# Another order for the attention stage's buffers, and the softmax denominators' sum on GpSimd

## The chip, the cores and the metric

The kernel runs on one core of one Trainium2 chip, in one launch. The metric is the device time in microseconds (us), as the median of several runs; less is better. The engines are named as in the profile: PE (TensorE matmul), PEld (its weight loads), DVE (VectorE), ACT (ScalarE), POOL (GpSimd), SP (SyncE, which here only issues DMAs). A suffix q, as in SPq, marks the engine's own queue.

## The reference

Two layers over 2048 latent tokens and 256 context tokens, width 1024, all in float32. Layer 0 is a gated spatial mixer. Layer 1, which the change touches, is windowed attention with 16 query heads and 4 key/value heads of 64:

```
s_loc = q·k over the block and one block to each side (|i-j| <= 128), masked
s_ctx = q·k_ctx over all 256 context keys
p     = softmax([s_loc, s_ctx, sink])          # one sink logit for each head
o     = p_loc @ v + p_ctx @ v_ctx
x     = LN(alpha*x + gate * ((o * silu(z)) @ w_out))
```

The softmax's denominator of a row and head is the sum of its exponentials (`l` in the kernel) and the exponential of the sink logit, both taken against the row's extreme value (`nm`).

## The kernel before, in words

**Stages.** The gated mixer and its output projection, then a projection stage that makes q, k, v and z of layer 1 and writes them to DRAM scratch, then attention with the output projection and the last LayerNorm. Each float32 matmul is made of three (or two) matmuls of split operands, high and low parts; the splitting (`hi_act` at L122 on ACT, `lo_dve` at L125 on DVE, `lo_pool` at L128 on POOL) follows every product of PE that is multiplied again.

**Attention.** There are 16 blocks of 128 queries (`b`), and in each four units, one for each key/value head (`kv`), of four query heads (`hq`). A unit goes over its key tiles `j`: three local ones and two of the context, so 5 steps (4 in the first and the last block). A block is thus 20 steps. For each unit: `s_mm` (L1100 to L1103) makes the scores, `s_max` (L1111, DVE) masks them and takes the extreme, `s_exp` (L1119, ACT) the exponentials and their sum `l`; for each step `t_mm` (L1126) transposes four heads' tile on PE, `t_hi` (ACT) and `t_lo` (DVE, tile `pl`) split it, `pv_mm` (L1143, L1144) multiplies it with v two steps later. `o_copy` (L1149, ACT) and `o_add` (L1155, DVE) end a unit.

**The denominators.** They are made for half a block at a time (`hf`: units 0 and 1, or 2 and 3), by `z_den`. Stage 0 (L1166, DVE) subtracts, stage 1 (L1168, ACT) takes the sink's exponential, stage 2 adds `l` (L1170), takes the reciprocal (L1171) and transposes it (L1173), all on DVE, stores it to DRAM scratch `escr` (L1175) and loads it back spread over the partitions as `eb` (L1179), both through SP. The last stage multiplies z with it on POOL (L1182). Then `y_mul` (L1187, POOL) multiplies the attention output with z, `y_hi` (ACT) and `y_lo` (L128, POOL, tile `yl`) split it, and `out_piece` (L1220 to L1222, PE) projects it, spread over the block that follows. `fin` is the LayerNorm of a finished block; its stage 5 is L579 on ACT, and its stage 6 is two additions and multiplications of a whole 128x1024 tile on POOL (L582, L583) with the store of the result.

**The order.** Each of these calls is put on a list with a time in steps (`at(t, fn, ...)`), and the list, sorted by time, is the order in which PE, DVE, ACT and POOL each get their instructions; an engine does not pass one instruction by for another. SP's order is left to the framework. In a block of 20 steps, counted from its first step, `z_den` stage 2 stands at 5.65 (first half) and 15.65 (second half), `t_lo` at .8 and `s_max` at .9 of a step, `o_add` at 6.5, 11.5, 16.5 and 21.5, stage 6 of `fin` for the block before the last one at 5.25, `y_lo` of the first half at 19.1, and the first `out_piece` that uses it at 21.4, which is 1.4 in the next block.

**The buffers.** A `Region` is a row of buffer groups, laid out in SBUF in the order of its list. The attention stage's region `b2` lies over what the projection stage used: first, from byte 0, 14 buffers of 4 KB (`bigb`) that hold the projection's split inputs `kh` and `kl` of the last token groups, which PE reads until the stage's last matmul; from 56 KB on the region `a3` (gate, hT, xt0 and xt1 of 4 KB each, then yr, yh, yl, tmp, whe, wle of 2 KB tiles). A new tile waits for the users of the earlier tiles on its own bytes. What attention needs first from DRAM are the keys of unit 1 (`kw` tiles, loads L1087 and L1088), v (`vk`), q, and a last weight row with its gate (both in `x1`). The scores of unit 0 are made already in the projection stage.

Of the kernel before, what the change touches and what calls it, by code (L numbers as in the profile page):

```python
# [12 lines left out]
ALU = mybir.AluOpType  # L13
# [36 lines left out]
def kernel(  # L50
# [28 lines left out]
    V, S, G, T = nc.vector, nc.scalar, nc.gpsimd, nc.tensor  # L79
# [69 lines left out]
    def kk_of(g):  # L149
        return 4 if GROUPS[g][1] == 256 else 2  # L150
# [9 lines left out]
    def at(th, g, k):  # L160
        return th[g, k // kk_of(g)][:, k % kk_of(g)]
# [312 lines left out]
    def spatial(c, g, cd, ut, vh, vl):  # L474
        tn = GROUPS[g][1]
        wsT, add = cd["wsT"], cd["add"]
        gc = gcols[:, c:c + 1]
        yt = a2.tile([P, tn], F32, "y", f"y{c}_{g}")
        npr = tn // 256
        pss = [bank(f"psp{c}_{g}_{pr}") for pr in range(npr)]  # L480
        for j in range(2):
            for pr in range(npr):
                T.matmul(pss[pr][:, j * 256:j * 256 + 256], vh[:, pr * 2 + j],
                         wsT.rearrange("q s p -> q (s p)"), start=True, stop=False)
            for pr in range(npr):
                T.matmul(pss[pr][:, j * 256:j * 256 + 128], vl[:, pr * 2 + j], wsT[:, 0], start=False, stop=True)
        for pr in range(npr):
            psv = pss[pr].rearrange("p (j s t) -> p j s t", j=2, s=2)
            t1 = a2.tile([P, 2, P], F32, "t1", f"t1{c}_{g}_{pr}")
            V.scalar_tensor_tensor(t1, psv[:, :, 1], gc, add[:, :].unsqueeze(1).broadcast_to([P, 2, P]),  # L490
                                   op0=ALU.mult, op1=ALU.add)
            V.scalar_tensor_tensor(t1, psv[:, :, 0], gc, t1, op0=ALU.mult, op1=ALU.add)
            cs = slice(pr * 256, pr * 256 + 256)
            G.tensor_tensor(yt[:, cs], t1.rearrange("p j t -> p (j t)"), ut[:, cs], op=ALU.mult)
        return yt
# [28 lines left out]
    for si, (c, g) in enumerate(steps):  # L524
# [16 lines left out]
        if si > 0:  # L541
            pc, pg = steps[si - 1]
            yt = spatial(pc, pg, cds[pc], uzs[si - 1], *vprep[si - 1])
# [370 lines left out]
    t = 0.0  # L914
# [88 lines left out]
    for n in range(1, 5):  # L1003
# [3 lines left out]
        for k in range(KD):  # L1007
            e = s + step * (k + 1) + 0.1
# [11 lines left out]
    with tc.manual_schedule(engines=compute | {mybir.EngineType.SP}):  # L1020
        for _, _, fn, a in sorted(plan, key=lambda p: p[:2]):
# [5 lines left out]
    b1.close()  # L1027
    bigb.close()

    b2 = Region(tc, "b2", [("kw", 4), ("x1", 2), ("otmp", 2), ("vk", 5), ("S", 9), ("ph", 7), ("q", 2), ("z", 1),  # L1030
                           ("eb", 2), ("pl", 7), ("oT", 2), ("yh0", 1), ("yh1", 1), ("yl0", 1), ("yl1", 1), ("yt", 2),
                           ("nm", 2), ("l", 2), ("es", 2), ("et", 2)])
    psS = ctx.enter_context(tc.tile_pool(name="psS", bufs=2, space=PSUM, reuse_waits="tile"))
    psT = ctx.enter_context(tc.tile_pool(name="psT", bufs=2, space=PSUM, reuse_waits="tile"))
# [2 lines left out]
    def b2t(name, shape, tag, bufs=None, dt=F32):  # L1037
        return b2.tile(shape, dt, tag, name)
# [15 lines left out]
    def len_keys(b):  # L1054
        return 4 if b in (0, NB - 1) else 5
# [105 lines left out]
    def z_den(b, hf, stage):  # L1161
        d = blk[b]
        es = est[hf][:, 0:8].rearrange("p (e j) -> p j e", e=2)
        nm, ns, l = (t[:, 8 * hf:8 * hf + 8].rearrange("p (j e) -> p j e", e=2) for t in (d["nm"], nsink, d["l"]))
        if stage == 0:
            V.tensor_tensor(es, nm, ns, op=ALU.subtract)  # L1166
        elif stage == 1:
            S.activation(est[hf][:, 0:8], est[hf][:, 0:8], AF.Exp)  # L1168
        elif stage == 2:
            V.tensor_tensor(es, es, l, op=ALU.add)  # L1170
            V.reciprocal(est[hf][:, 0:8], est[hf][:, 0:8])  # L1171
            et = b2t(f"et{b}_{hf}", [P, 32], "et")
            V.transpose(et, est[hf])  # L1173
            scr = escr[2 * b + hf]
            ld(scr.rearrange("i h q -> (i h) q"), et)  # L1175
            d["eb", hf] = eb = b2t(f"eb{b}_{hf}", [P, 4, P], "eb")
            for e in range(2):
                src = scr[:, 4 * e:4 * e + 4].rearrange("i j q -> i (j q)").unsqueeze(0)
                ld(eb[64 * e:64 * e + 64], src.broadcast_to([64, 4, P]))  # L1179
        else:  # L1180
            z = d["z"][:, 4 * hf:4 * hf + 4].rearrange("p j (i q) -> p j i q", i=4)
            G.tensor_tensor(z, z, d["eb", hf].rearrange("p i (j q) -> p j i q", j=4), op=ALU.mult)  # L1182
# [148 lines left out]
    for b in range(NB):  # L1331
        e = block_step[b + 1] if b + 1 < NB else NS
        if b + 1 < NB:
            at(block_step[b] + 8, load_block, b + 1)
        at(e - 11, z_load, b)
        for hf in range(2):
            if hf and b == NB - 1:
                break
            zb = first_step[4 * b + 2 * hf] + 3.55
            for i, t in enumerate((0.15, 1.1, 2.1)):  # L1340
                at(zb + t, z_den, b, hf, i)
            at(zb + 4.6 if hf else e - 7, z_den, b, hf, 3)
        if b == NB - 1:
            continue
        for hf in range(2):
            z = e + (-2.1 if len_keys(b) == 5 else -1.6, 1.9)[hf]
            ks = (4 * hf, 4 * hf + 4)
            at(z + (-3, -0.1)[hf], y_mul, b, *ks)
            at(z + (0.7, 1.5)[hf], y_hi, b, *ks)
            at(z + (1.2, 2.0)[hf], y_lo, b, *ks)  # L1350
        o = e + (1.4 if len_keys(b) == 5 else 1.7)
        os = 1.2 if b < NB - 2 else 0.8
        for i in range(2 * KD):
            at(o + i * os + (0.3 if i >= KD else 0), out_piece, b, i)
        for hf in range(2):
            t = o + (KD * (hf + 1) - 1) * os + hf * 0.3
            at(t + 0.3, out_copy, b, hf)
            at(t + 0.8, out_add, b, hf)
            at(t + 2.3, fin, b, hf)
        t += 2.35  # L1360
        late = (1.1, 2.8, 3.2) if b < NB - 2 else (0.5, 0.6, 0.7)
        for i, dt in enumerate((0, 0.3) + late):
            at(t + dt, fin, b, 2 + i)
    b, e = NB - 1, NS
    for i, t in enumerate((-5.05, -4.7, -4.0, -1.6)):
        at(e + t, z_den, b, 1, i)
    at(e - 2.3, y_mul, b, 0, 4)
    at(e - 1.9, y_hi, b, 0, 4)
# [84 lines left out]
```

## Time and profile before

| | |
|---|---|
| median of 3 runs | 2802.15 us (2800.67 to 2805.03) |
| the profiled execution, its own time | 2803.22 us |
| its span, first to last instruction | 2801.4 us |
| attention, from 2160 us on | 641.4 us of the span |

The profile shows one execution. Its time is 1.07 us above the median, and 1.82 us of it lie around the span. Stretches are given in us from the span's start; attention's first blocks lie at 2160 to 2204, its even part (blocks of about 39.6 us) at 2204 to 2757, its end behind that.

### The profile page before, as it was taken

How to read it: one execution, taken by the hardware profiler on the slowest of the kernel's cores; microseconds unless marked ns; L12 is line 12 of the kernel's file. 1: busy time of each engine (PE TensorE's matmuls, PEld its weight loads, DVE VectorE, ACT ScalarE, POOL GpSimd, SP SyncE). 2: the span in 40 equal slices, each digit the busy share in tenths (PEclk: the TensorE clock that was granted, in tenths of full speed). 3: DMA queues.
4: the chain of work that ended last, by engine and by line, in shares of the span. 5: the costliest groups of instructions: out<-in, count | busy, mean ns of one | idle time of the engine just before them, and what ended most of it. 6: DMA issues, size and time to landing. Idle time of an engine off the chain costs nothing.

```text
span 2801.4 us, 37614 instructions
## 1 busy us (share of the span) xinstructions
PE 2745.6 (98%) x13896; PEld 2323.9 (83%) x13896; DVE 1625.0 (58%) x3210; ACT 948.8 (34%) x1863; POOL 642.0 (23%) x522
## 2 busy tenths in 40 slices
PE   6999999999999999999999999999999999999998
PEld 4788888888888888888888888888888888888887
DVE  8612214666556665556545555545424888888887
ACT  4411211112211211223111112322213777777775
POOL 6000001322222222221011112122100334333343
PEclk9999999999999999999999999999999999999999
DMA  6422312322322322236333336633334544444442
GB/s 226 147 76 83 89 53 80 101 80 90 112 82 84 101 92 80 83 97 194 101 117 113 114 126 208 215 128 116 114 130 139 155 132 131 120 130 124 131 121 69
DMA packets 280717, 328.06 MB, mean 117 GB/s; under 512 B 24275, under 2 KB 192595, under 8 KB 280534
## 3 DMA queue, kind: packets, MB, share of 16 engines
q1 hardware_dynamic: 241652, 305.61, 34.0%
q10 hardware_dynamic: 38882, 20.05, 2.5%
q8 instruction: 109, 1.79, 0.3%
q14 instruction: 74, 0.61, 0.1%
HBM read 221.76 MB, written 103.83 MB: 116 GB/s over the span
## 4 chain that ended last, share of the span: by engine, by line
PE 87%; DVE 6%; DMA 3%; ACT 1%; issue 1%; POOL 0%; SPq 0%; DVEq 0%; ACTq 0%; POOLq 0%
PE pu L380 5%; PE pu L381 5%; PE pu L382 5%; PE pz L381 5%; PE pz L382 5%; PE pz L380 5%; PE po L622 5%; PE po L623 5%; PE po L625 5%; PE pt L744 4%; PE pt L745 4%; PE pt L743 4%; PE pv L244 4%; PE pv L242 4%; PE pv L243 4%; PE pT L1126 4%
## 5 line engine op out<-in xcount | busy, mean ns | idle before, releaser
L125 DVE TENSOR_TENSOR pl<-pT,ph 128x512 fp32r<-128x512 f32 x312 | 214.4, 687 | 78.4 <-ACT ph L122 74.6
L242 PE MATMUL pv<-wvh,hh 128*128 128x512 f32 x576 | 229.1, 398 | 16.5 <-ACT hh L122 16.5
L380 PE MATMUL pu<-hh,wuh 128*128 128x512 f32 (+1 forms) x640 | 240.4, 376 | 0.0
L381 PE MATMUL pu<-hh,wul 128*128 128x512 f32 (+1 forms) x640 | 236.1, 369 | 0.0
L382 PE MATMUL pu<-hl,wuh 128*128 128x512 f32 (+1 forms) x640 | 235.7, 368 | 0.0
L380 PE MATMUL pz<-hh,wzh 128*128 128x512 f32 (+1 forms) x640 | 235.4, 368 | 0.0
L381 PE MATMUL pz<-hh,wzl 128*128 128x512 f32 (+1 forms) x640 | 235.4, 368 | 0.0
L382 PE MATMUL pz<-hl,wzh 128*128 128x512 f32 (+1 forms) x640 | 235.4, 368 | 0.0
L244 PE MATMUL pv<-wvh,hl 128*128 128x512 f32 x576 | 229.2, 398 | 5.6 <-DVE hl L125 5.6
L622 PE MATMUL po<-woh,yh 128*128 128x512 f32 x576 | 226.7, 394 | 2.6 <-ACT yh L122 2.6
L743 PE MATMUL pt<-kh,wbh 128*128 128x512 f32 (+1 forms) x592 | 228.8, 386 | 0.0
L744 PE MATMUL pt<-kh,wbl 128*128 128x512 f32 (+1 forms) x592 | 228.7, 386 | 0.0
L745 PE MATMUL pt<-kl,wbh 128*128 128x512 f32 (+1 forms) x592 | 228.6, 386 | 0.0
L243 PE MATMUL pv<-wvl,hh 128*128 128x512 f32 x576 | 227.7, 395 | 0.0
L623 PE MATMUL po<-wol,yh 128*128 128x512 f32 x576 | 225.0, 391 | 0.0
L625 PE MATMUL po<-woh,yl 128*128 128x512 f32 x576 | 221.8, 389 | 0.0
L471 POOL TENSOR_TENSOR u<-u,z 128x512 f32<-128x512 f32 (+1 forms) x80 | 107.8, 1348 | 487.2 <-DVE z L470 479.0
L1111 DVE CUSTOM_DVE_ANT_0 S<-pS,mask 128x640 f32<-128x640 f32 (+1 forms) x252 | 216.9, 861 | 2.5 <-PE pS L1103 2.5
L1119 ACT ACTIVATE S<-S,nm 128x640 f32<-128x640 f32 (+1 forms) x240 | 196.7, 819 | 56.5 <-DVE nm L1111 56.5
L122 ACT ACTIVATE ph<-pT 128x512 fp32r<-128x512 f32 x312 | 185.0, 593 | 69.3 <-PE pT L1126 67.3
L1126 PE MATMUL pT<-ident,S 128*128 128x128 f32 x1232 | 186.0, 273 | 10.5 <-DVE pl L125 8.4
L470 DVE SCALAR_TENSOR_TENSOR z<-z,pz 128x512 f32<-128x512 f32 (+1 forms) x80 | 50.5, 632 | 243.1 <-ACT z L469 243.0
(235 smaller groups left out, 6142.0 us busy)
## 6 DMA issues: line engine op xcount, KB each, us to landing
vscr<-vt ACTq DMA_DIRECT2D x72, 256.0 KB, 2.3
yr<-yscr SPq DMA_DIRECT2D x72, 256.0 KB, 3.1
ar<-in_dram SPq DMA_DIRECT2D x64, 256.0 KB, 2.7
vr<-vscr SPq DMA_DIRECT2D x64, 256.0 KB, 2.7
yscr<-y SPq DMA_DIRECT2D x64, 256.0 KB, 2.5
q<-qscr SPq DMA_DIRECT2D x64, 256.0 KB, 3.8
wor<-in_dram SPq DMA_DIRECT2D x46, 256.0 KB, 2.7
kh<-khscr SPq DMA_DIRECT2D x56, 192.0 KB, 3.7
```

The source lines that it names most:

```text
L242: T.matmul(ps, hk[:, cs], wh, start=first, stop=False)
L243: T.matmul(ps, hk[:, cs], wl, start=False, stop=False)
L244: return T.matmul(ps, lk[:, cs], wh, start=False, stop=last)
L380: T.matmul(ps[:, 0:tn], w[0][:, k], at(hh, g, k), start=(k == 0), stop=False)
L381: T.matmul(ps[:, 0:tn], w[1][:, k], at(hh, g, k), start=False, stop=False)
L382: T.matmul(ps[:, 0:tn], w[0][:, k], at(hl, g, k), start=False, stop=(k == KD - 1))
L622: T.matmul(pss[hf], hi[:, c % 4], wh[:, cs], start=(c == 0), stop=False)
L623: T.matmul(pss[hf], hi[:, c % 4], wl[:, cs], start=False, stop=False)
L625: T.matmul(pss[hf], lo[:, c % 4], wh[:, cs], start=False, stop=(c == NC_A - 1))
L743: T.matmul(ps, wh[:, cs], at(kh, g, k), start=(k == 0), stop=False)
L744: T.matmul(ps, wl[:, cs], at(kh, g, k), start=False, stop=False)
L745: T.matmul(ps, wh[:, cs], at(kl, g, k), start=False, stop=(k == KD - 1))
```

## The change

The list of `b2` is put in another order: S, ph, pl, otmp and yt, which engines write, come first, over `bigb`; kw, vk, x1 and q, which DMAs write, come to lie from 58.5 to 90.5 KB, over `a3`. The sizes stay. In `z_den` the addition of `l` goes from DVE to POOL and stays at its place in the list as stage 2; the reciprocal, the transposition and the DMAs become stage 3, 0.9 steps later (6.55 and 16.55 in a block of 20 steps); the multiplication by POOL becomes stage 4, and for the second half goes from 18.15 to 18.85. In the last block the addition goes from -4.0 to -4.2 steps before the end and the rest to -3.9.

```diff
-    b2 = Region(tc, "b2", [("kw", 4), ("x1", 2), ("otmp", 2), ("vk", 5), ("S", 9), ("ph", 7), ("q", 2), ("z", 1),
-                           ("eb", 2), ("pl", 7), ("oT", 2), ("yh0", 1), ("yh1", 1), ("yl0", 1), ("yl1", 1), ("yt", 2),
+    b2 = Region(tc, "b2", [("S", 9), ("ph", 7), ("pl", 7), ("otmp", 2), ("yt", 2), ("kw", 4), ("vk", 5), ("x1", 2),
+                           ("q", 2), ("z", 1), ("eb", 2), ("oT", 2), ("yh0", 1), ("yh1", 1), ("yl0", 1), ("yl1", 1),
                            ("nm", 2), ("l", 2), ("es", 2), ("et", 2)])
...
         elif stage == 2:
-            V.tensor_tensor(es, es, l, op=ALU.add)
+            G.tensor_tensor(es, es, l, op=ALU.add)
+        elif stage == 3:
             V.reciprocal(est[hf][:, 0:8], est[hf][:, 0:8])
...
-            for i, t in enumerate((0.15, 1.1, 2.1)):
+            for i, t in enumerate((0.15, 1.1, 2.1, 3.0)):
                 at(zb + t, z_den, b, hf, i)
-            at(zb + 4.6 if hf else e - 7, z_den, b, hf, 3)
+            at(zb + 5.3 if hf else e - 7, z_den, b, hf, 4)
...
-    for i, t in enumerate((-5.05, -4.7, -4.0, -1.6)):
+    for i, t in enumerate((-5.05, -4.7, -4.2, -3.9, -1.6)):
         at(e + t, z_den, b, 1, i)
```

## Rows read from the trace of the kernel before

**Rows 1.** Stretches: us, busy us of PE, PEld, DVE, ACT, POOL; granted clock, DMA.
```profile
2160.00:2204.00 44.00, 36.97 (x226) 30.96 (x225) 34.84 (x79) 32.59 (x73) 12.52 (x8) 0.96 0.75 230
2204.00:2757.00 553.00, 544.62 (x3252) 474.71 (x3251) 480.49 (x1025) 429.23 (x881) 213.34 (x152) 1.00 0.41 123
```
**Rows 2.** Waits of PE, 2205 to 2770: us in total, times, longest.
```profile
PE pT L1126 <- DVE pl L125: 8.4, 13, 0.7
PE pO L1144 <- DVE pl L125: 0.6, 1, 0.6
```
**Rows 3.** Groups by line, DVE, 2205 to 2757: busy us, mean ns, idle before.
```profile
L1170 DVE TENSOR_TENSOR es<-es,l 128x8 f32<-128x8 f32 x28 | 32.4, 1158 | 0.0
```
**Rows 4.** The same view, POOL, 2205 to 2757.
```profile
L583 POOL TENSOR_TENSOR x<-x,st 128x1024 f32<-128x1024 f32 x13 | 30.9, 2378 | 1.0
L566 POOL TENSOR_TENSOR brs<-brs,mhalf 128x1 f32<-128x1 f32 x14 | 7.7, 551 | 16.7 <-DVE brs L562 16.7
```
**Rows 5.** Timeline, a first half: start, us, engine, line, [idle before, releaser].
```profile
2520.55 2.40 POOL L582 TENSOR_TENSOR x<-x,st 128x1024 f32<-128x1024 f32 x1 [2.26 <-ACT x L579]
2520.68 2.30 DVE L1170 TENSOR_TENSOR es<-es,l 128x8 f32<-128x8 f32 x1
2522.13 0.60 ACT L1149 ACTIVATE ot<-pO 64x512 f32<-64x512 f32 x1
2523.02 0.20 DVE L1171 RECIPROCAL es<-es 128x8 f32<-128x8 f32 x1
2523.03 2.38 POOL L583 TENSOR_TENSOR x<-x,st 128x1024 f32<-128x1024 f32 x1
2523.39 0.65 DVE L125 TENSOR_TENSOR pl<-pT,ph 128x512 fp32r<-128x512 f32 x1
2524.09 0.66 PE L1126 MATMUL pT<-ident,S 128*128 128x128 f32 x4 [0.66 <-DVE pl L125]
2526.57 0.39 PE L1144 MATMUL pO<-pl,v 128*128 128x512 f32 x1
```
**Rows 6.** Timeline, a second half, to the first use of `yl`.
```profile
2501.21 0.17 DVE L1170 TENSOR_TENSOR es<-es,l 128x8 f32<-128x8 f32 x1
2501.89 0.33 SPq L1175 DMA_DIRECT2D escr<-et  x1
2503.34 0.85 DVE L1155 TENSOR_TENSOR oT<-pO,ot 64x256 f32<-64x256 f32 x2
2507.94 1.29 POOL L1182 TENSOR_TENSOR z<-z,eb 128x512 f32<-128x512 f32 x1 [11.97 <-DMA eb<-escr]
2509.23 1.29 POOL L128 TENSOR_TENSOR yl<-oT,yh 128x512 fp32r<-128x512 f32 x1
2512.70 0.40 PE L1222 MATMUL pY<-wobh,yl 128*128 128x512 f32 x1
```
**Rows 7.** Timeline, `yl` and its first use one block earlier.
```profile
2471.35 1.31 POOL L128 TENSOR_TENSOR yl<-oT,yh 128x512 fp32r<-128x512 f32 x1
2473.12 0.40 PE L1222 MATMUL pY<-wobh,yl 128*128 128x512 f32 x1
```
**Rows 8.** Timeline where attention begins.
```profile
2160.40 0.32 SPq L1087 DMA_DIRECT2D kh<-khscr  x1
2161.26 0.69 DVE L836 SCALAR_TENSOR_TENSOR zt<-zt,pt 128x512 f32<-128x512 f32 x1 [3.76 <-ACT zt L834]
2162.74 0.36 PE L1100 MATMUL pS<-kh,q 128*128 128x256 f32 x1 [2.15 <-DMA kh<-khscr]
2163.41 0.58 PE L1101 MATMUL pS<-kl,q 128*128 128x256 f32 x1 [0.32 <-DMA kl<-klscr]
2164.46 0.75 DVE L1111 CUSTOM_DVE_ANT_0 S<-pS,mask 128x512 f32<-128x512 f32 x1 [2.51 <-PE pS L1103]
```
**Rows 9.** Stretch just behind: columns as in rows 1.
```profile
2163.00:2166.50 3.50, 3.18 (x15) 3.09 (x15) 1.32 (x3) 1.19 (x3) 0.00 (x0) 0.51 0.90 309
```
**Rows 10.** Timeline, waits inside the first block.
```profile
2174.33 0.95 DVE L1170 TENSOR_TENSOR es<-es,mask 128x8 f32<-128x8 f32 x1
2176.39 0.50 PE L1144 MATMUL pO<-pl,v 128*128 128x512 f32 x1 [1.50 <-DVE pl L125]
2201.06 0.63 ACT L122 ACTIVATE yh<-oT 128x512 fp32r<-128x512 f32 x1 [1.16 <-POOL oT L1187]
2202.96 0.50 PE L1144 MATMUL pO<-pl,vc 128*128 128x512 f32 x1 [0.20 <-DVE pl L125]
```

## The prediction

> **What bounds the kernel now.** I read the stretches first, then PE's waits, then the groups by line, then the timelines of one block, of the start of attention and of its first block. In attention's even part PE is busy for 544.6 of 553 us [rows 1]: what PE does not wait for cannot be won there. The list of its waits is short: 13 waits of up to 0.7 us and one of 0.6 us, 9.0 us together, all for `pl` of DVE [rows 2]. The reason stands in the groups: 28 additions of 128x8 numbers take 32.4 us [rows 3], though one takes 0.17 us [rows 6]. The timeline shows which are the long ones: the addition of the first half begins 0.13 us after POOL's L582 and ends with it, 2.30 us later [rows 5]. Half of them are like this; with 2.13 us lost in each, 28 x 0.17 + 13 x 2.13 = 32.5 us. Behind it `pl` comes late and PE idles 0.66 us [rows 5]. At the start of attention PE idles 2.15 and 0.32 us for the keys' loads, the first of which SP could issue only at 2160.40, behind the projection's last matmul [rows 8], and then runs for 3.5 us at a granted 0.51 [rows 9], the lower of the clock's two levels (1.2 GHz).
>
> **The layout.** The first keys come to lie over gate, hT and xt0, whose last readers are stores of z that the code issues well before the stage's last matmul; v and q lie on bytes that are free by then or soon after. The loads then land before PE is through, and the 2.15 and 0.32 us go. PE is through 2.15 us before 2162.74, at 2160.6. The first score tile takes two of the eight PSUM banks that the projection used, and L836 reads one of those banks until 2161.95 [rows 8]. If the tile lies on that bank, PE begins at about 2162.0, if not at 2160.6. I take the bank, since each of the last tiles had a bank of its own and the new tile takes two. From PE's first score matmul to DVE's start it took 1.72 us, 0.32 of it the wait and the rest mostly at half clock [rows 8, 9], so about 0.7 us at full clock: DVE starts at 2162.7 instead of 2164.46, 1.8 us earlier. The tiles that now lie over `bigb` cost nothing: S, ph and pl are written behind matmuls that follow the last reader on PE itself.
>
> **The first block.** There DVE sets the pace (PE waits 1.50 us for it [rows 10]), so its lead counts, and the addition of 0.95 us goes too, of which 0.78 is stall: 1.8 + 0.8 = 2.6 us won. The second half's denominators lose some of this: the reciprocal now follows one `pl` and one scores instruction, 0.65 and 0.75 us [rows 5, 8], less 0.17 for the addition that is gone, 1.2 us, and the chain behind it, store, load, two multiplications, already ends in a wait of ACT for `oT` that PE feels with 0.20 us [rows 10]. So -2.6 + 1.2 = **-1.4 us** for the start. Ends: -3.5, if PE begins at 2160.6 and its clock doesn't fall; +0.5, if the lead is lost again and only the longer chain stays.
>
> **The addition on POOL, first half.** It stays at 5.65 in the list, and on POOL both instructions of `fin` stage 6 stand at 5.25. So it queues behind L582 and also behind L583, which ends at 2525.41 [rows 5]. No row shows a POOL addition of 8 columns. From 1.29 us at 512 columns [rows 6] and 2.38 at 1024 [rows 4] a straight line gives 2.1 ns a column and 0.2 us fixed: 0.22 us. Bounds are DVE's own 0.17 [rows 6] and the 0.55 of a one-column power on POOL [rows 4]. I take 0.22, the same operation. The addition is done at 2525.67. DVE meanwhile runs on: `pl` and scores of step 5 and `o_add`, whose ACT copy ends at 2522.73 [rows 5] and which takes 0.85 us [rows 6], are through by 2523.65. Then comes the reciprocal, and DVE stands until 2525.70: 2.05 us, in place of the 2.13 that it lost before. Behind it queue the transposition and `pl` of step 6, which starts 0.37 us after the reciprocal does [rows 5] and takes 0.69: it ends at 2526.75. What is late next is L1144, which needs that `pl`: it ran at 2526.57, and without the old wait would run at 2525.91 [rows 5]. It will run at 2526.79: a wait of 0.88 us in place of 0.66. That is 0.22 us more for each of 14 blocks (13 in the even part, one in the last block): **+3.1 us**. With the bounds, 0.17 to 0.55 us a block: +2.4 to +7.7.
>
> The Trainium skill, GPSIMD Engine Reference, section Engine selection, advises against this move: an elementwise addition belongs on VectorE, GpSimd being about 2x slower for two inputs. By that the addition would take 0.34 us here and the sum would be 1.7 us higher; no run here shows that length yet.
>
> **The reciprocal moved, second half.** Here nothing collided before: the addition took 0.17 us and the store of the transposed reciprocals was issued at 2501.89 [rows 6]. At 16.55 the reciprocal now stands behind `pl`, the scores and `o_add` of 16.5, which ends at 2504.19 [rows 6]; reciprocal and transposition end 0.45 us later, at 2504.64, where before they ended at 2501.86: 2.8 us late. Every step behind is late with them: the store to `escr`, the loads of `eb` that wait for its landing, the multiplication of z (2507.94, 6.05 us behind the store's issue), and POOL's next instruction, `y_lo` of the first half [rows 6]. That the multiplication's place went from 18.15 to 18.85 changes nothing: it still stands ahead of `y_lo` (19.1). `yl` was ready at 2510.52 and PE's first use of it, L1222, ran at 2512.70 [rows 6]: 2.18 us of cover. In the block before it was 0.46 [rows 7]. Read over the fourteen blocks in this way, seven have 2.1 to 2.3 us, two 1.9, two 1.2, three 0.5 to 0.8: 1.7 in the mean. So PE waits 2.8 - 1.7 = 1.1 us in each of 14 blocks: **+15.4 us**. Ends: 0.5 us each, if all loads are as quick as in rows 6 (+7), and 2.3 each, if all are as slow as in rows 7 (+32). SP's other loads (keys, v) that may stand behind the later store are for scores four steps on, and I cost them at nothing; if that cover is gone, they stall PE at its next scores. POOL's additions for the second half find POOL idle (11.97 us before L1182 [rows 6]) and cost nothing, and DVE's 0.17 us saved there only lengthens its wait for ACT.
>
> **Sum.** -1.4 + 3.1 + 15.4 = +17.1 us on the profiled execution's 2803.2 us gives 2820.3; the median is 1.07 us lower, so 2819.2, which I round to 2820.
>
> **The rivals.**
> *The delay is covered.* If store and loads take 0.5 us less than in rows 6, or `y_lo` finds more cover, only -1.4 + 3.1 is left: 2804. For it speaks that in half of the blocks only 0.5 us is lacking; against it that the other half lacks 0.9 to 2.3.
> *Faster.* The addition on POOL no longer stalls DVE, because it is done when the reciprocal comes up. Then all 14 x 0.66 = 9.2 us come back, with 1.4 at the start: 2792, if the second half is covered as well. It decides at 2523.65: POOL would have to be free 1.8 us earlier than its two instructions of 2.4 us let it [rows 5], for instance by DVE reaching that point later. Against it stands the order of the list.
> *The clock falls too.* A wait of 2.15 and 0.32 us was followed by 3.5 us at half clock [rows 9], which costs some 1.7 us; the one of 1.50 us [rows 10] wasn't followed by a fall, as the 0.96 of the whole stretch [rows 1] is that one fall (3.5 x 0.49 of 44 us). Should each of the 14 new waits do this: +24 us, 2844; should only the three longest do it: 2825.
> *The layout does nothing,* because the scores wait for something else at 2162.7: 2822, inside the forecast's own range.
>
> **How the numbers follow.** Chances: forecast 0.66 (its own range 2808 to 2832), clock 0.10, covered 0.15, faster 0.09. A measurement of this kernel can tell about 0.2%, 5.6 us. Slower is forecast and clock, 0.76; no difference is the covered case, 0.15; faster 0.09. The range of 2803 to 2836 holds the forecast, the covered case and the lower part of the clock's, and leaves out about 0.14.
>
> **What would show it.** In the profile after: no DVE instruction of 128x8 longer than 0.3 us; POOL's 128x8 addition right behind L583 in 14 blocks, of about 0.2 us; DVE idle about 2 us ahead of the reciprocal, released by POOL; PE's waits for `pl` still there, at L1144 instead of L1126, of 0.9 us; new waits of L1222 for `yl` of POOL, 0.5 to 2.3 us, once a block; at the start the first scores at about 2162.0. The prediction is wrong if the waits for `yl` are missing, if POOL's addition runs ahead of L582, or if the blocks' length doesn't grow from 39.6 us (the two L1222 of rows 6 and 7) to about 40.9.

## The result, and the profile after

The kernel after takes 2825.52 us (median of 6 runs, 2824.22 to 2828.72), the kernel before, run beside it, 2803.59. The ratio is 1.0082, with a 95% interval of 1.0071 to 1.0092: slower by 0.8%, about 22 us. Forecast were 2820 us, 2803 to 2836, and slower.

The profiled execution took 2826.38 us, with a span of 2824.6. From L1171 on every line number is one higher than before: the reciprocal is L1172, the transposition L1174, the store to `escr` L1176, the load of `eb` L1180, the multiplication of z L1183, the use of `yl` L1223.

PE's waits in attention, 2150 to 2825 us (in total, times, longest), are to be laid beside [rows 2, 8, 10]. Two more, of 2.2 us for `S` and of 1.1 us for the `yl` of DVE, are as long as before, to 0.1 us:

```profile
PE pY L1223 <- POOL yl L128: 16.6, 14, 2.1
PE pO L1144 <- DVE pl L125: 12.2, 18, 1.2
PE pO L1143 <- DMA v<-vkscr: 4.4, 1, 4.4
PE pS L1100 <- issue: 1.5, 1, 1.5
```

The first line is new: one wait for `yl` a block. The second stands where the waits of [rows 2] stood, somewhat longer. The third is new too, and was not forecast: the first v. The waits of L1100 and L1101 for the keys [rows 8] are gone. The same matmuls in the even part (x3252 in both) now take 576 us in place of 553 [rows 1]:

```profile
2204.00:2780.00 576.00, 549.23 (x3252) 474.16 (x3251) 451.10 (x997) 427.22 (x881) 217.53 (x179) 1.00 0.40 118
```

**A first half**, timeline, to be read beside [rows 5]:

```profile
2532.25 2.40 POOL L582 TENSOR_TENSOR x<-x,st 128x1024 f32<-128x1024 f32 x1 [2.83 <-ACT x L579]
2534.51 0.85 DVE L1155 TENSOR_TENSOR oT<-pO,ot 64x256 f32<-64x256 f32 x2
2534.72 2.40 POOL L583 TENSOR_TENSOR x<-x,st 128x1024 f32<-128x1024 f32 x1
2537.08 0.21 POOL L1170 TENSOR_TENSOR es<-es,l 128x8 f32<-128x8 f32 x1
2537.33 0.20 DVE L1172 RECIPROCAL es<-es 128x8 f32<-128x8 f32 x1 [1.97 <-POOL es L1170]
2537.70 0.65 DVE L125 TENSOR_TENSOR pl<-pT,ph 128x512 fp32r<-128x512 f32 x1
2538.41 0.50 PE L1144 MATMUL pO<-pl,v 128*128 128x512 f32 x1 [0.78 <-DVE pl L125]
```

POOL's addition waits out both long instructions, DVE stands 1.97 us in front of the reciprocal, `pl` is late behind it, and PE pays 0.78 us. The groups of 2205 to 2780 us say that this is the rule (idle time before the group behind the second bar; POOL's addition, then DVE's reciprocal):

```profile
L1170 POOL TENSOR_TENSOR es<-es,l 128x8 f32<-128x8 f32 x27 | 5.8, 214 | 45.3 <-ACT es L1168 45.3
L1172 DVE RECIPROCAL es<-es 128x8 f32<-128x8 f32 x28 | 5.7, 203 | 26.0 <-POOL es L1170 25.6
```

**A second half**, timeline, beside [rows 6]:

```profile
2515.21 0.33 SPq L1176 DMA_DIRECT2D escr<-et  x1
2517.24 1.27 SPq L1180 DMA_DIRECT2D eb<-escr  x2
2521.88 1.30 POOL L1183 TENSOR_TENSOR z<-z,eb 128x512 f32<-128x512 f32 x1 [11.21 <-DMA eb<-escr]
2522.98 0.40 PE L1222 MATMUL pY<-wobl,yh 128*128 128x512 f32 x1
2523.13 1.27 POOL L128 TENSOR_TENSOR yl<-oT,yh 128x512 fp32r<-128x512 f32 x1
2524.45 0.50 PE L1223 MATMUL pY<-wobh,yl 128*128 128x512 f32 x1 [1.07 <-POOL yl L128]
2524.79 0.34 PE L1100 MATMUL pS<-kh,q 128*128 128x384 f32 x1
2565.42 0.50 PE L1223 MATMUL pY<-wobh,yl 128*128 128x512 f32 x1 [1.01 <-POOL yl L128]
```

POOL had been idle for 11 us and stood for `eb`; `yl` was ready 1 us after PE wanted it. From one such wait to the next it is 40.97 us, a block, in place of 39.6 [rows 6, 7].

The same place before, around the L1222 of [rows 6]:

```profile
2512.47 0.40 PE L1221 MATMUL pY<-wobl,yh 128*128 128x512 f32 x1
2512.94 0.33 PE L1100 MATMUL pS<-kh,q 128*128 128x384 f32 x1
```

From the last matmul ahead of `yl` to the first score behind it, it took 0.47 us; now it takes 1.81. That is 1.34 us more, though the wait is listed with 1.07: a listed wait begins where the matmul ahead of it ends, while without a wait the next matmul starts before that end (at 2512.70, not 2512.87), and the matmul behind the wait takes 0.10 us longer. All fourteen waits for `yl` cost 0.26 to 0.27 us beyond what is listed.

**Where attention begins**, timeline, beside [rows 8]:

```profile
2156.68 0.53 SPq L1159 DMA_DIRECT2D z<-zscr  x1
2158.27 1.20 SPq L880 DMA_DIRECT2D q<-qscr  x2
2158.90 0.69 DVE L836 SCALAR_TENSOR_TENSOR zt<-zt,pt 128x512 f32<-128x512 f32 x1 [3.76 <-ACT zt L834]
2159.51 0.62 SPq L1274 DMA_DIRECT2D gate<-gscr  x1
2159.69 0.36 PE L1100 MATMUL pS<-kh,q 128*128 128x256 f32 x1 [1.46 <-issue]
2160.17 1.07 SPq L1047 DMA_DIRECT2D v<-vkscr  x2
2160.44 0.75 DVE L1111 CUSTOM_DVE_ANT_0 S<-pS,mask 128x512 f32<-128x512 f32 x1 [0.85 <-PE pS L1103]
2168.08 0.77 PE L1143 MATMUL pO<-ph,v 128*128 128x512 f32 x1 [4.42 <-DMA v<-vkscr]
```

Before, the first v was issued ahead of the keys, and PE did not wait for it:

```profile
2159.04 0.32 SPq L1047 DMA_DIRECT2D v<-vkscr  x1
2168.01 0.40 PE L1143 MATMUL pO<-ph,v 128*128 128x512 f32 x1
```

After, PE's first scores run 0.10 us behind the end of L836 (2159.59), and DVE takes them 1.54 us behind L836's start, before 3.20 [rows 8]. But both v are issued behind z, q and gate, and PE stands 4.42 us for the first of them. The granted clock in the two stretches behind is below 1:

```profile
2166.50:2170.00 3.50, 1.92 (x5) 1.41 (x6) 0.00 (x0) 0.00 (x0) 0.00 (x0) 0.71 0.95 314
2170.00:2173.00 3.00, 3.00 (x19) 2.73 (x18) 1.35 (x3) 1.56 (x4) 2.38 (x1) 0.77 0.33 94
```

To see what the first block lost, I take DVE's first subtraction for block 1 (L1166). It runs at 2200.62, 41.7 us behind L836, before 2200.38 and 39.1 us. The stages ahead of L836 are the same in both kernels, yet over all the kernels of this study L836 started anywhere from 2156.9 to 2161.8 us. So single executions are compared from L836 on: 640.1 us to the end of the span before, 665.7 after, a loss of 25.6. (The whole of the profiled execution lost 23.2, since L836 started 2.4 us earlier in it.)

### The profile page after: what moved, and what is told of

It is laid out like the page before. It is cut to its first block, busy times and chain, and to the rows that moved or that the text cites. A ratio compares the mean times of both kernels' runs of the same rounds, so it can differ in the third digit from the quotient of the medians.

```text
span 2824.6 us, 37599 instructions
## 1 busy us (share of the span) xinstructions
PE 2750.0 (97%) x13896; PEld 2322.8 (82%) x13896; DVE 1594.4 (56%) x3178; ACT 946.7 (34%) x1863; POOL 646.7 (23%) x554
```

## The experiments

Each kernel was timed against the kernel before on the same chip. Waits are of one profiled execution, 2150 to 2825 us; "attention" is its span less the start of L836.

| kernel | median us | ratio to before (95%) | waits for `yl` of POOL, `pl`, v | attention |
|---|---|---|---|---|
| before | 2803.59 | | none, 11.6, none | 640.1 |
| after | 2825.52 | 1.0082 (1.0071 to 1.0092) | 16.6, 12.2, 4.4 | 665.7 |
| layout_alone | 2805.54 | 1.0011 (1.0002 to 1.0019) | none, 10.4, 3.9 | 643.4 |
| sum_alone | 2829.11 | 1.0096 (1.0083 to 1.0110) | 19.7, 14.2, none | 672.1 |
| recip_early_2nd | 2810.56 | 1.0028 (1.0017 to 1.0039) | none, 13.4, 3.9 | 645.5 |
| add_ahead | 2812.66 | 1.0035 (1.0023 to 1.0047) | 18.1, 1.0, 5.0 | 653.4 |
| both_new | 2792.85 | 0.9961 (0.9948 to 0.9973) | none, 1.4, 4.3 | 630.6 |
| both_old | 2794.07 | 0.9960 (0.9946 to 0.9973) | none, 4.0, none | 632.1 |
| dve_ahead_old | 2790.21 | 0.9955 (0.9941 to 0.9968) | none, 1.1, none | 628.9 |
| both_v4 | 2790.49 | 0.9953 (0.9941 to 0.9966) | none, 1.4, 1.9 | 628.7 |
| ylo_first | 2808.06 | 1.0015 (1.0006 to 1.0024) | none, 13.4, 3.9 | 646.7 |
| add_dve | 2822.03 | 1.0072 (1.0059 to 1.0086) | 19.9, 1.2, 3.8 | 661.1 |
| dve_ahead_v4 | 2792.11 | 0.9961 (0.9948 to 0.9973) | none, 1.1, 1.7 | 627.7 |
| add_dve_early2 | 2802.21 | 0.9999 (0.9990 to 1.0008) | none, 3.7, 3.8 | 639.1 |

**The two parts apart.** The kernel before with only the new list of `b2`:

> The kernel before with only the new order of the buffers. As predicted (the keys land early, DVE starts sooner, the lead stays): about 2 us less than before, 2801.5. By the trace after (v is now issued behind z, q and gate, PE's first L1143 waits about 4.4 us for it and the clock falls behind that wait, so the lead is lost): 0 to 3 us more than before, 2803.5 to 2806.5, with one wait of 3 to 5 us for v and the even part's 9 us of waits for pl as before, none for yl. Rival, that the layout is what costs the time (SP's order delays the later loads too): 2815 or more, with waits for yl.

The kernel after with the old list:

> The kernel after with the old order of the buffers: only the addition on GpSimd and the moved steps. Theory (the two terms of the moved denominators): +3 for the waits for pl and +15 to +17 for the waits for yl, 2821 to 2824, no long wait for v. Rival, that the layout makes most of the loss: 2808 or less.

The layout alone costs 0.11%, 2 to 3 us, and shows the wait for v, no wait for `yl`, and about the same 8.5 us for `pl` as before:

```profile
PE pT L1126 <- DVE pl L125: 8.5, 13, 0.7
```

All that it loses, it loses in the first block: from L836 to the first L1166 of block 1 it takes 42.4 us for 39.1, and from there to the end of the span 601.0 us in both. So the layout isn't the loss, and it isn't the small gain that I forecast either. The sum alone came out at 2829.1, 5 us above the theory's upper end. Its profiled execution was the slowest of the four, 2832.97 us. In it the waits for `yl` were 19.7 instead of 16.6, PE stood 1.61 us for a load of kh in the first block (2190.68), and the clock fell behind this wait and behind two of the longer ones for `yl`, of 2.19 and 2.11 us (and, as in after, behind the last one, here the longest with 2.40 us, at 2777.08). The windows there (columns as in [rows 1]):

```profile
2190.60:2194.00 3.40, 3.32 (x11) 2.77 (x12) 2.53 (x6) 1.19 (x4) 1.11 (x1) 0.54 0.51 185
2237.90:2241.00 3.10, 3.10 (x14) 3.06 (x15) 1.75 (x5) 0.62 (x2) 2.41 (x2) 0.62 0.00 0
2446.00:2449.00 3.00, 3.00 (x15) 2.76 (x14) 2.39 (x7) 1.93 (x4) 2.28 (x3) 0.64 0.22 59
```

By an estimate, time by the clock that was lacking, they lose 3.4 x 0.46 + 3.1 x 0.38 + 3.0 x 0.36 = 3.8 us. Why `yl` comes later over the old list I did not settle.

**The reciprocal of the second half.** Put back behind the addition, the multiplication of z left at its new place:

```diff
-            for i, t in enumerate((0.15, 1.1, 2.1, 3.0)):
+            for i, t in enumerate((0.15, 1.1, 2.1, 2.15 if hf else 3.0)):
```

> The kernel after, but in the second half of each block the reciprocal, transposition and their transfers stand right behind the addition again; the multiplication of z keeps its new place 18.85. Theory (the late store and loads make yl late): the 16.6 us of waits for yl go to under 2 us, those for pl stay at about 12, time 2809 to 2812. Rival, that the later place of the multiplication on GpSimd makes yl late: the waits stay, 2823 to 2827. Rival, that what is won at yl turns up as another wait of PE (for eb, oT or pl): the waits for yl go and the time stays above 2818.

And the other way round, the reciprocal left late and only the multiplication put behind the `y_lo` of the first half:

```diff
-            at(zb + 5.3 if hf else e - 7, z_den, b, hf, 4)
+            at(zb + 5.7 if hf else e - 7, z_den, b, hf, 4)
```

> The kernel after, but the second half's multiplication of z goes from 18.85 to 19.25, behind the y_lo of the first half (19.1); the reciprocal and its transfers stay late at 16.55. Theory (y_lo is late only because GpSimd takes its instructions in order and the multiplication ahead of it waits for eb): the 16.6 us of waits for yl go to under 2 us, time 2808 to 2812, as with the reciprocal put back. Rival, that the late eb then delays the second half's own y_mul and yl, which PE needs some steps later: new waits at L1223 or later, 2818 or more.

Each alone takes all waits for `yl` away; 15.0 and 17.5 us come back. One block's timeline with the multiplication moved shows the queue turned round:

```profile
2510.41 1.30 POOL L128 TENSOR_TENSOR yl<-oT,yh 128x512 fp32r<-128x512 f32 x1 [9.08 <-ACT yh L122]
2512.53 1.29 POOL L1183 TENSOR_TENSOR z<-z,eb 128x512 f32<-128x512 f32 x1 [0.82 <-DMA eb<-escr]
2515.16 1.30 POOL L1188 TENSOR_TENSOR oT<-z,oT 128x512 f32<-128x512 f32 x1
```

`yl` no longer stands behind a multiplication that waits for `eb`, and the multiplication still ends 1.3 us before the `y_mul` that needs it. The rival that the later place of the multiplication was the cause fell with the first run; the rival of a new wait in its place fell with both, but for 1.2 us more for `pl`.

**The addition of the first half.** On POOL, but ahead of `fin` stage 6 instead of behind it:

```diff
-            for i, t in enumerate((0.15, 1.1, 2.1, 3.0)):
+            for i, t in enumerate((0.15, 1.1, 2.1 if hf else 1.15, 3.0)):
```

> The kernel after, but the first half's addition on GpSimd stands at 4.70 in the list, ahead of the two long instructions at 5.25, instead of 5.65 behind them. Theory (the addition waits in GpSimd's queue behind L582 and L583, DVE stands for it, pl comes late): the 12.2 us of waits for pl go to under 3 us, DVE's reciprocal no longer waits, those for yl stay at 16 to 17, time 2813 to 2817. Rival, that DVE is slowed by GpSimd's long instructions in any order (the stall passes to the next DVE instruction): waits for pl of 8 us or more stay, 2821 or more.

The waits for `pl` go from 12.2 to 1.0, those for `yl` grow by 1.5, and 12.9 us come back, all that the theory asked for. So the stall does not pass on to another instruction of VectorE. Then the engine by itself: every place in the list kept, the addition on DVE again (`V` for `G` in stage 2).

> The kernel after with the additions back on VectorE and every place in the list kept. Theory (the engine of the addition is worth only the 3 us of the queue behind L583, the rest is the moved reciprocal): the long additions of 2.3 us are back in the first halves, waits for pl about 9 us in place of 12.2, those for yl of 16 to 18 stay, 2820 to 2825, 0 to 5 us less than after. Rival, that GpSimd's addition itself makes the loss: 2810 or less.

The time fell as expected, by 3.5 us, but for another reason. The group of the additions shows that they collide with L582 as before, and PE hardly waits for `pl`:

```profile
L1170 DVE TENSOR_TENSOR es<-es,l 128x8 f32<-128x8 f32 x27 | 32.1, 1189 | 0.0
```
```profile
PE pO L1144 <- DVE pl L125: 1.2, 5, 0.4
```

Two causes were open for that: `pl` no longer stands behind the reciprocal and transposition, or the waits for `yl` give DVE its lead. The run that tells them apart takes the waits for `yl` away too:

> The kernel after with the additions back on VectorE and, in the second half, the reciprocal right behind the addition: of the change only the order of the buffers and the first half's later reciprocal are left. It asks why the waits for pl vanished where the addition on VectorE still took 2.3 us. Theory (pl no longer stands behind the reciprocal and the transposition, 0.37 us, which leaves about 0.3 of the 0.66 us): waits for pl of 3 to 5 us, 2799 to 2802. Rival, that the 1.4 us for which PE stood for yl a few steps earlier gave VectorE its lead, and the place of the reciprocal nothing: waits for pl of about 9 us, 2804 to 2807. Rival, that 0.37 us is all it takes: under 1.5 us, 2795 to 2799.

The waits for `pl` in the blocks' first halves are 2.1 us in 11, against 8.5 in 13 in layout_alone, with the reciprocal in its old place. (The 1.6 of the second line are not at that place: the 1.9 of layout_alone stand in the same line.)

```profile
PE pT L1126 <- DVE pl L125: 2.1, 11, 0.2
PE pO L1144 <- DVE pl L125: 1.6, 4, 0.9
```

So the late reciprocal by itself is worth most of the old waits, here 6.4 us of waits and 3.3 us of time, a little more than the 0.37 us a block that the theory counted; the lead from `yl` isn't needed for it.

**Both undone, and better.** Both moves together, the addition of the first half at 4.70 and the reciprocal of the second at 15.70, over the new list and over the old:

```diff
-            for i, t in enumerate((0.15, 1.1, 2.1, 3.0)):
+            for i, t in enumerate((0.15, 1.1, 2.1, 2.15) if hf else (0.15, 1.1, 1.15, 3.0)):
```

> The kernel after with both moves: the first half's addition on GpSimd ahead of its two long instructions, and the second half's reciprocal right behind the addition. Theory (the two waits are separate and all of the loss): waits for pl and yl of GpSimd both gone, 12 and 16 us less than after, 2796 to 2800, faster than before by about 0.15 to 0.25 % because the 9 us of waits for pl that before had are gone too, less the 3 us that the layout costs. Rival, that the two waits cover each other in part (one won turns up in the other): 2803 or more.

> The same two moves on the old order of the buffers. Theory (the layout alone costs 2 to 3 us by the late load of v): 2794 to 2797. Rival, that the new layout saves time where the sum is on GpSimd (as the 3.6 us between the sum alone and the kernel after would say): 2800 to 2804.

Together they give back 32.7 us, more than 15.0 + 12.9 and 3 us more than the theory's best case, part of it because each wait had grown by 1.2 to 1.5 us when the other was gone. Old and new list can't be told apart here (0.9960 and 0.9961), so that the layout costs 2 to 3 us is not shown in this pair. In the profiled execution over the old list POOL's queue took its toll once more, in the first block, where the addition stood behind a multiplication that waited (and the `y_mul` behind it, L1188), and DVE stood 2.93 us for it:

```profile
2189.56 1.28 POOL L1183 TENSOR_TENSOR z<-z,eb 128x512 f32<-128x512 f32 x1 [11.28 <-DVE oT L1155]
2192.13 0.21 POOL L1170 TENSOR_TENSOR es<-es,mask 128x8 f32<-128x8 f32 x1
2192.38 0.20 DVE L1172 RECIPROCAL es<-es 128x8 f32<-128x8 f32 x1 [2.93 <-POOL es L1170]
```

Then the kernel before, with one number changed. DVE keeps the addition, with the reciprocal and transposition right behind it, and the first half's goes from 5.65 to 4.85, ahead of a scores instruction:

```diff
-            for i, t in enumerate((0.15, 1.1, 2.1)):
+            for i, t in enumerate((0.15, 1.1, 2.1 if hf else 1.3)):
```

> The kernel before, with one number changed: the first half's addition stays on VectorE and goes from 5.65 to 4.85 in the list, one scores instruction earlier, with the reciprocal and transposition behind it. Theory (the 2.30 us of the addition is its overlap with L582 on GpSimd and nothing else, so its place decides, not its engine): VectorE's addition takes 0.17 us in all blocks, the 9 us of waits for pl go, 2793 to 2796. Rival, that the scores instruction now collides in its place or that pl comes late in any case: 2800 or more.

2790.21 us, 0.45% faster than before and 3 us below the theory's range. One block's timeline, and the group of all:

```profile
2511.74 0.16 DVE L1170 TENSOR_TENSOR es<-es,l 128x8 f32<-128x8 f32 x1
2512.41 2.41 POOL L582 TENSOR_TENSOR x<-x,st 128x1024 f32<-128x1024 f32 x1 [2.27 <-ACT x L579]
```
```profile
L1170 DVE TENSOR_TENSOR es<-es,l 128x8 f32<-128x8 f32 x28 | 4.7, 167 | 0.1
```
```profile
2204.00:2760.00 556.00, 556.00 (x3339) 486.55 (x3338) 466.17 (x1051) 442.41 (x908) 221.04 (x156) 1.00 0.42 125
```

The addition is over before L582 begins; 28 of them take 4.7 us where they took 32.4 [rows 3]; PE is busy for all of these 556 us.

**The wait for v.** In the new list, `vk` behind `z`, so that SP's order becomes v, q, v, z, gate; once with both moves and once with DVE's addition ahead:

```diff
-... ("yt", 2), ("kw", 4), ("vk", 5), ("x1", 2),
-                           ("q", 2), ("z", 1), ("eb", 2), ...
+... ("yt", 2), ("kw", 4), ("x1", 2), ("q", 2), ("z", 1),
+                           ("vk", 5), ("eb", 2), ...
```

> The kernel after with both moves and the v buffers behind z in the new order, so that the first v is issued ahead of z, q and gate. Theory (PE's wait of 4 to 5 us for v and the fall of the clock behind it come from the order of the loads): no wait for v, the first block keeps its lead, 2791 to 2796 and 3 to 5 us less than the same without this. Rival, that DVE or ACT sets the first block's pace anyway: within 1 us of the kernel without this, 2796 to 2800.

> The kernel before with the first half's addition on VectorE at 4.85 and the new order of the buffers with the v buffers behind z. Theory (layout and addition are separate; with v early the new order of the buffers is worth the 2 us at the keys' loads, as predicted for the layout): 2787 to 2790, up to 3 us less than with the old order (2790.2). Rival, that the first block's lead is lost again to v, which still came 1.9 us late in this order: 2789.5 to 2793, no difference to be told.

The wait fell from 4.3 to 1.9 us, and is now for the second v, which stands behind q; attention fell by 1.9 (630.6 to 628.7). In the medians that is 2.4 us, and the intervals overlap; the 3 to 5 us expected weren't reached. Over DVE's early addition this list gives no difference that the times can tell (0.9961 against 0.9955). Of the kernels that are faster than before, dve_ahead_old is the one with the smallest change, and none beats it measurably.

## Why the prediction came out

**The whole.** Three runs lead from before to after in four steps. Each step is one part of the change; the second also holds the multiplication of z at its new place and the changed places of the last block. Their medians give the change's price by parts: the layout +2.5 (2803.0 to 2805.5), the first half's late reciprocal -3.3 (to 2802.2, with the addition still on DVE), the additions to POOL +8.4 (to 2810.6), the second half's late reciprocal +15.0 (to 2825.5). The medians of before beside them were 2803.0, 2802.1, 2803.0 and 2803.6, so each step is good to about 2 us; with each run taken against the before beside it, the steps are +2.5, -2.5, +7.5 and +14.4.

**The reciprocal moved, second half: +15.4 forecast, right.** The waits are 16.6 us in 14, 0.52 to 2.10 each, for the bounds of 0.5 to 2.3; undoing it gives 15.0 us back. The chain is the one named: late store, late `eb`, a multiplication of z that waits, and `y_lo` behind it. The two runs show that it takes both links, the late `eb` and the queue. The store comes 2.9 us late for PE: it was issued 10.8 us ahead of PE's use of `yl` before (2501.89 to 2512.70 [rows 6]) and 7.9 after (2515.21 to 2524.45, less the 1.34 us). 2.8 us were forecast.

The mean of the waits came out, 1.19 us for 1.1, but not their spread. By the cover that was read, seven blocks should have waited 0.5 to 0.7 us and three 2.0 to 2.3; in fact eleven waits lie between 0.9 and 1.4 us. The forecast asked only whether PE would miss SP's other loads, and not whether they would hold up `eb`. Before, SP issued nothing between this store and the load of `eb`, and in ten of the fourteen blocks the load followed 1.42 to 1.48 us behind the store (1.42 in the block of [rows 6]). In after kh, kl and mostly v are issued between the two, and it is mostly 2.03 us. The one block with the shortest wait, 0.52 us, has 1.56. So quick blocks waited longer and two of the three slow ones shorter than by the forecast; that this nearly cancels in the mean was luck.

The rival that the delay would be covered fell: the least wait was 0.52 us.

**The addition on POOL, first half: +3.1 forecast, right as a net, too coarse as an account.** In the even part the waits for `pl` are 0.78 us in each of 13 blocks, 10.1 us, for 8.4 before [rows 2] and 0.88 a block forecast; behind it they are 1.5 us for 0.9. That is +2.3 us. DVE stood 1.97 us (2.05 forecast), and POOL's addition takes 0.214 us (0.22). But I set the new stand of DVE against the old stall as if only the engine differed. In fact the late reciprocal had already taken most of the old wait away, and POOL's queue put it back with more: -3.3 and +8.4, a net of +5.1 in the medians.

The Trainium skill, GPSIMD Engine Reference, section Engine selection, puts GpSimd about 2x behind VectorE for an addition of two inputs. At this size the trace shows 214 ns against 167, 1.28x, so the measurement differs from the figure; its advice against the move came true here, but by the queue.

**The start: -1.4 forecast, the step that failed.** Its first half held: scores began 0.10 us behind L836, as they would if the tile lies on its bank (the trace names no releaser, but the distance is 0.09 to 0.11 us in layout_alone, both_v4 and dve_ahead_v4 too), and DVE came 1.66 us earlier relative to L836 (1.8 forecast). The sentence "v and q lie on bytes that are free by then or soon after" was the mistake. I asked when the bytes come free and not in which order SP would then issue its loads; with the new list v stands behind z, q and gate, which PE needs later. It was issued 2.2 us ahead of L836's start before and 1.3 us behind it after, 3.5 us later. PE's first multiplication with v, L1143, runs 9.2 us behind L836's start instead of 6.8. These 2.4 us later, at the end of the wait of 4.4 us, are nearly all of the 2.6 by which the first block is longer; forecast was 1.4 shorter, and 0.5 longer at worst. The lower clock is no new loss: 3.5 x 0.29 + 3.0 x 0.23 = 1.7 us behind this wait, for 3.5 x 0.49 = 1.7 before [rows 9], both estimates. The layout alone costs 2.5, and with v earlier the wait shrinks. As the list moves the bytes together with the order, no run here shows whether v's bytes would have been free sooner.

**The clock.** The rival that it falls behind each new wait did not come true: the even part is at 1.00 in the mean. It fell at v, and once more, behind the last wait for `yl` (2.10 us at 2770.72), in these stretches (from 2764 to 2768 it was at 1.00):

```profile
2770.70:2774.00 3.30, 3.28 (x16) 2.95 (x17) 1.73 (x5) 0.50 (x2) 2.83 (x3) 0.71 0.00 0
2774.00:2778.00 4.00, 4.00 (x21) 3.36 (x20) 2.97 (x6) 2.27 (x6) 1.45 (x2) 0.81 0.64 197
```

That is 3.3 x 0.29 + 4 x 0.19 = 1.7 us. The new wait of 1.63 us, at 2483.44, was not followed by a fall.

**The sum.** Start +2.6, `pl` in the even part +1.7 and behind it +0.6, `yl` 16.6, the clock at the end 1.7: 23.2 of the 25.6 us from L836 on. The rest is what a wait costs beyond what is listed. A block less its listed waits takes 40.97 - 1.01 - 0.78 = 39.18 us (2524.45 to 2565.42), and before 39.58 - 0.62 = 38.96 (2473.12 to 2512.70 [rows 6, 7], with one wait for `pl`): 0.22 us more, in fourteen blocks 3.1, an estimate. With it the sum is 26.3, 0.7 too much.

The forecast's +17.1 is 8.5 us short of these 25.6: 4.0 at the start, 1.2 in the listed waits for `yl`, 1.7 for the clock, and 2.4 for what is not listed, less 0.8 at `pl`. That the medians differ by 21.9 us, only 5 from the forecast, is luck in part: in the profiled executions 2.4 us lie ahead of L836, in stages that the change doesn't touch.

**The faster rival** needed POOL's addition to be done when the reciprocal comes up. In after it never was; in add_ahead it was, by one place in the list, and 11 us of waits went. The mechanism was right, its condition was not met by this change.

## What to carry to other kernels

An instruction that is moved to another engine joins that engine's queue. Before moving 0.2 us of work, read what stands ahead of it there and who waits behind; here the same addition one instruction earlier, on its old engine, was worth 0.45%. A step at the head of a long chain (store, load, multiply, split) has its slack at the chain's end: read that slack block by block before putting the step later, and look at what else the queue that issues its transfers will put in between. And a new buffer layout is also a new order of loads: read which load is now issued behind which.

## What the runs showed of the hardware

**A short addition can last as long as a neighbour's long one.** DVE's 128x8 addition of two SBUF operands took 2.30 us from 0.13 us behind the start of L582 on [rows 5], 2.29 in add_dve, and 0.16 when it ran 0.67 us ahead of it. `pl`, with one operand in PSUM, takes 0.65 us under L583 [rows 5] and 0.69 under L582 (in after, at 2533.09). By the Trainium skill, SBUF — State Buffer, section SBUF: two separate sides, the two engines share a port pair that one instruction holds to its end, and a VectorE instruction with two SBUF inputs takes part in it; the traces agree.

**Behind some waits of 1.6 to 2.4 us the granted clock fell, behind others as long it didn't.** It was at 0.54 to 0.71 in some 3 us that followed, between its two levels of 1.2 and 2.4 GHz (0.50 and 1.00): at 2190.68, 2237.90 and 2445.40 in sum_alone, 2770.72 in after. The wait of 1.77 us for `yl`, in add_ahead at 2478.48, was followed by this:

```profile
2478.40:2482.00 3.60, 3.52 (x15) 3.39 (x16) 2.29 (x7) 1.44 (x4) 2.84 (x4) 0.63 0.04 9
```

That is 3.6 x 0.37 = 1.3 us on top of the wait. Length alone doesn't decide: behind the 1.61 us in sum_alone it fell, behind 1.63 us in after it didn't. In add_dve it stayed at 1.00 behind a wait for `yl` of 2.68 us (2480.23), longer than any for `yl` behind which it fell, and was at 0.65 in the 3 us behind one of 2.01 (2765.05).

**A short wait costs more than the profile lists.** Each of the fourteen waits for `yl` in after put the next score off by 0.26 to 0.27 us more than its listed time (0.52 to 2.10 us), since the matmuls before and behind it no longer overlap, as the lines of the second half show.
